# Moving one small store between queues and adding unread products at the end of a row-maximum kernel

## Chip, cores, metric

One core of a Trainium2 chip. The metric is device time in microseconds (us) of one execution; medians are over executions on the chip. Profiles are single executions; "the span" is the profiled part of one, about 1.8 us shorter than its time.

## The reference

```python
def setup_inputs():
    return {"x": np.random.randn(8192, 8192).astype(np.float32)}

def reference(x):
    return np.linalg.norm(x, ord=np.inf, axis=1)   # the largest |x| of each row
```

It is 268 MB in and 32 KB out.

## The kernel before

SyncE loads pairs of rows for each of the 128 partitions into a ring of three 64 KB buffers, and VectorE reduces them to one value for each row, in columns of `res`. The last rows come in shrinking pieces, shared by VectorE, ScalarE (absolute value) and GpSimd (maximum). At the end TensorE turns the columns of `res` into lines by a transpose against the identity, ScalarE copies them out of PSUM, and two stores write them out: 60 row tiles as "pairs", and the last 4 as "ones", which contain the row tile that is reduced last. So that TensorE's clock is up for these transposes, products that nobody reads (`ps_warm`) are issued near the end; `WARM` gives their lengths in blocks of 128 columns by tile (negative) or by piece of the last tile.

```python
WARM = {-2: (4, 4, 4), -1: (4,), 0: (4,), 1: (2,)}
# ...
    def warm(after, widths):
        for w in widths:
            not_before(
                keep(nc.tensor.matmul(
                    ps_warm[:, : w * P], lhsT=ident,
                    rhs=ident.unsqueeze(1).to_broadcast([P, w, P]), start=True, stop=True,
                )),
                after, "not before this piece",
            )
# ... in the loop over the pieces of all tiles
            if final:                                    # the last piece of the last tile
                for r in range(2):
                    keep(nc.scalar.copy(sb_pairs[:, :, r], ps_pairs[r]))
                absmax(res[:, R - 1 :], last)            # the last reduction, VectorE
            elif u == len(TILES) - 1:                    # an earlier piece h of the last tile
                if h == 0:
                    # ... two transposes into ps_pairs
                red = shared(last, w_last + n_part, buf, w, g)
                n_part += 1 + len(g)
                warm(red, WARM.get(h, ()))
# ... after the loop
    nc.tensor.transpose(ps_ones, res[:, X_ONE:], ident)
    keep(nc.scalar.copy(sb_ones, ps_ones))
    keep(nc.scalar.dma_start(
        out=out[X_ONE * P :].rearrange("(r p) -> r p", p=P), in_=sb_ones
    ))
    nc.sync.dma_start(
        out=out[: X_ONE * P].rearrange("(g p r) -> g p r", p=P, r=2), in_=sb_pairs
    )
```

## Time and profile before

| | before |
|---|---|
| time | 628.23 us (3 runs, 628.09 to 628.24) |
| DMA engines busy | 99% of the span, 428 GB/s |
| VectorE busy | 536.8 us (86%) |
| last reduction ends | 623.87 us into the span |
| from there to the end of the span ("the tail") | 2.75 us |

The lines are shown in the prediction. They are read in this order: the chain of work that ended last, to see that loads and reductions make up 99% of it; the timeline of the last 4 us, to see the serial path of the tail and what lies beside it; the granted clock in narrow slices, to see what TensorE ran at. The tail serves below as the measure of each change: the load stream ahead of it ends at a different moment in each execution (623.49 to 623.87 us in the ten profiles without a changed last store), which hides tenths of a microsecond in the total time but not in the tail.

### The profile page before, as it was taken

What the parts mean: (1) busy time and instruction counts of PE and PEld (TensorE: products, weight loads), DVE (VectorE), ACT (ScalarE), POOL (GpSimd) and SP (SyncE); (2) the same over time, 40 slices, a digit from 0 to 9 for tenths busy, and PEclk for the clock granted to TensorE, in tenths of its full rate; (3) what the DMA queues carried; (4) which work ended last, traced back from release to release, by engine and by line L of the source; (5) the groups of instructions that cost most, each with busy time, mean ns of one, the idle gap of its engine ahead of it and who ended that gap; (6) DMA issues with size and microseconds to landing.
All of it is one profiled execution on the core that took longest, in us unless ns stands there. A gap on an engine that the chain in (4) does not pass through costs nothing.

```text
span 626.6 us, 212 instructions
## 1 busy us (share of the span) xinstructions
PE 8.1 (1%) x15; PEld 3.0 (0%) x15; DVE 536.8 (86%) x40; ACT 15.6 (2%) x13; POOL 14.6 (2%) x16
## 2 busy tenths in 40 slices
PE   0000000000000000000000000000000000000005
PEld 0000000000000000000000000000000000000001
DVE  1938988889888899888898888988889888899888
ACT  0000000000000000000000000000000000000044
POOL 0000000000000000000000000000000000000026
PEclk9999999999999999999999999999999999999999
DMA  8999999999999999999999999999999999999997
GB/s 368 435 469 402 469 402 469 402 469 402 464 406 464 406 456 414 431 439 427 443 410 460 406 464 402 469 402 469 402 464 406 464 406 464 406 460 410 439 410 291
DMA packets 5669, 268.47 MB, mean 428 GB/s; under 512 B 643, under 2 KB 933, under 8 KB 1317
## 3 DMA queue, kind: packets, MB, share of 16 engines
q1 hardware_dynamic: 5661, 268.47, 99.2%
q10 hardware_dynamic: 8, 0.00, 0.0%
HBM read 268.44 MB, written 0.03 MB: 428 GB/s over the span
## 4 chain that ended last, share of the span: by engine, by line
DMA 71%; DVE 28%; SPq 0%; issue 0%; PE 0%; ACT 0%; DVEq 0%
DMA ring<-in_x_dram 71%; DVE res L75 28%; DVE last L75 1%; SPq L147 0%; PE ps_ones L189 0%; ACT sb_ones L190 0%; DVEq L75 0%
## 5 line engine op out<-in xcount | busy, mean ns | idle before, releaser
L75 DVE TENSOR_REDUCE res<-ring 128x2 f32<-128x16384 f32 (+1 forms) x32 | 525.4, 16420 | 86.8 <-DMA ring<-in_x_dram 86.8
L97 ACT ACTIVATE ring<-ring 128x3712 f32<-128x3712 f32 (+7 forms) x8 | 13.5, 1712 | 575.9 <-DMA ring<-in_x_dram 572.6
L82 POOL TENSOR_REDUCE part<-ring 128x1 int32<-128x3712 int32 (+3 forms) x4 | 10.1, 2563 | 586.0 <-ACT ring L97 586.0
L118 PE MATMUL ps_warm<-ident 128*128 128x512 f32 (+1 forms) x12 | 7.5, 764 | 614.5 <-DVE part L75 613.2
L118 PEld LDWEIGHTS ps_warm<-ident 128*128 128x128 f32 x12 | 2.7, 258 | 618.4 <-issue 615.3
L75 DVE TENSOR_REDUCE part<-ring 128x1 f32<-128x800 f32 (+1 forms) x2 | 5.5, 2748 | 0.1
L75 DVE TENSOR_REDUCE last<-ring 128x1 f32<-128x2176 f32 (+4 forms) x5 | 5.3, 1115 | 0.1
L82 POOL TENSOR_REDUCE last<-ring 128x1 int32<-128x1696 int32 (+3 forms) x4 | 3.3, 842 | 0.5 <-ACT ring L97 0.4
L110 ACT ACT_TABLE_LOAD x1 | 1.3, 1283 | 31.6 <-DVE res L75 31.6
L104 POOL MEMSET ident<- 128x128 f32 x1 | 0.2, 206 | 21.5 <-DVE res L75 21.5
L75 DVE TENSOR_REDUCE res<-last 128x1 f32<-128x425 f32 x1 | 0.6, 595 | 0.1
L161 ACT COPY sb_pairs<-ps_pairs 30x128 f32<-30x128 f32 x2 | 0.4, 252 | 0.0
L82 POOL TENSOR_REDUCE res<-part 128x1 int32<-128x3 int32 x2 | 0.4, 200 | 0.1
L167 PE MATMUL ps_pairs<-ident,res 128*30 128x128 f32 x2 | 0.4, 272 | 0.0
L189 PE MATMUL ps_ones<-ident,res 128*4 128x128 f32 x1 | 0.3, 348 | 1.7 <-DVE res L75 1.7
masks.py:199 POOL TENSOR_SCALAR_AFFINE_SELECT ident<-ident 128x128 f32<-128x128 f32 x1 | 0.3, 295 | 0.1
L190 ACT COPY sb_ones<-ps_ones 4x128 f32<-4x128 f32 x1 | 0.3, 255 | 1.5 <-PE ps_ones L189 1.5
L167 PEld LDWEIGHTS ps_pairs<-ident,res 128*30 128x30 f32 x2 | 0.2, 106 | 0.6 <-issue 0.6
L110 ACT ACTIVATE ident<-ident 128x1 f32<-128x1 f32 x1 | 0.2, 203 | 0.0
L211 POOL MEMSET const-float32-0.0<- 128x1 f32 x1 | 0.1, 99 | 0.2 <-issue 0.2
L211 POOL MEMSET const-bfloat16-1.0<- 128x1 bf16 x1 | 0.1, 102 | 0.0
L211 POOL MEMSET const-uint8-127<- 128x1 uint8 x1 | 0.1, 102 | 0.0
(2 smaller groups left out, 0.2 us busy)
## 6 DMA issues: line engine op xcount, KB each, us to landing
ring<-in_x_dram SPq DMA_DIRECT2D x3, 4096.0 KB, 21.6
ring<-in_x_dram SPq DMA_DIRECT2D x1, 1936.0 KB, 35.4
ring<-in_x_dram SPq DMA_DIRECT2D x1, 976.0 KB, 37.3
ring<-in_x_dram SPq DMA_DIRECT2D x1, 512.0 KB, 38.1
ring<-in_x_dram SPq DMA_DIRECT2D x30, 40.8
ring<-in_x_dram SPq DMA_DIRECT2D x1, 272.0 KB, 38.3
last<-in_x_dram SPq DMA_DIRECT2D x1, 208.0 KB, 38.3
ring<-in_x_dram SPq DMA_DIRECT2D x1, 192.0 KB, 38.3
```

The lines of the kernel that those rows point to most:

```text
L75: return keep(nc.vector.tensor_reduce(out=dst, in_=src, axis=X, op=MAX, apply_absolute_value=True,))
L82: keep(pool.add_instruction(mybir.InstTensorReduce(name=nc.get_next_instruction_name(), ins=[pool.lower_ap(src.bitcast(INT32))], outs=[poo ...
L97: keep(nc.scalar.activation(buf[:, a : a + c], buf[:, a : a + c], ABS))
L104: not_before(nc.gpsimd.memset(ident, 0.0), after, "not before the first row is in")
L110: keep(nc.scalar.activation(ident[:, :1], ident[:, :1], ABS)),
L118: keep(nc.tensor.matmul(ps_warm[:, : w * P], lhsT=ident, rhs=ident.unsqueeze(1).to_broadcast([P, w, P]), start=True, stop=True,)),
L161: keep(nc.scalar.copy(sb_pairs[:, :, r], ps_pairs[r]))
L167: keep(nc.tensor.transpose(ps_pairs[r], both[:, :, r], ident))
L189: nc.tensor.transpose(ps_ones, res[:, X_ONE:], ident)
L190: keep(nc.scalar.copy(sb_ones, ps_ones))
L211: nc = _bacc.Bacc("TRN2", target_bir_lowering=False, num_devices=1)
```

## The change

The pairs' store goes from SyncE's queue to ScalarE's, ahead of the last store in program order. Two more unread products keep TensorE busy until just before the last transpose.

```diff
-WARM = {-2: (4, 4, 4), -1: (4,), 0: (4,), 1: (2,)}
+WARM = {-2: (4, 4, 4), -1: (4,), 0: (4,), 1: (2,), 2: (2,), 4: (1,)}
@@ in the loop, final piece
                 for r in range(2):
                     keep(nc.scalar.copy(sb_pairs[:, :, r], ps_pairs[r]))
+                keep(nc.scalar.dma_start(
+                    out=out[: X_ONE * P].rearrange("(g p r) -> g p r", p=P, r=2), in_=sb_pairs
+                ))
                 absmax(res[:, R - 1 :], last)
@@ after the loop
-    nc.sync.dma_start(
-        out=out[: X_ONE * P].rearrange("(g p r) -> g p r", p=P, r=2), in_=sb_pairs
-    )
```

## The prediction

> **What bounds the kernel now.** I read the page first (busy shares, then the chain of work that ended last), because it says whether the edited lines stand on the path at all.
>
> ```profile
> PE 8.1 (1%) x15; PEld 3.0 (0%) x15; DVE 536.8 (86%) x40; ACT 15.6 (2%) x13; POOL 14.6 (2%) x16
> ...
> DMA ring<-in_x_dram 71%; DVE res L75 28%; DVE last L75 1%; SPq L147 0%; PE ps_ones L189 0%; ACT sb_ones L190 0%; DVEq L75 0%
> ```
>
> The second line is the chain by tile and line: loads into the ring take 71% of it and the VectorE reductions that free the ring 28%. The DMA engines are busy 99% of the span at 428 GB/s, reading 268.44 MB; that stream alone is 268.44 / 0.428 = 627 us. Nothing in the edit touches it: the first added product waits for a reduction that ends at 622.3 us. So only the last 4 us can move, and I read those from the timeline, restricted to narrow windows, to see instructions singly.
>
> ```profile
> 622.42 0.41 ACT L161 COPY sb_pairs<-ps_pairs 30x128 f32<-30x128 f32 x2
> 622.85 0.42 SPq L194 DMA_DIRECT2D out_dram<-sb_pairs  x1
> 623.27 0.59 DVE L75 TENSOR_REDUCE res<-last 128x1 f32<-128x425 f32 x1
> 623.92 0.08 PEld L189 LDWEIGHTS ps_ones<-ident,res 128*4 128x4 f32 x1 [2.05 <-DVE res L75]
> 623.92 0.35 PE L189 MATMUL ps_ones<-ident,res 128*4 128x128 f32 x1 [1.65 <-DVE res L75]
> 624.31 0.26 ACT L190 COPY sb_ones<-ps_ones 4x128 f32<-4x128 f32 x1 [1.48 <-PE ps_ones L189]
> 624.60 0.55 ACTq L191 DMA_DIRECT2D out_dram<-sb_ones  x1
> ```
>
> Columns: start and duration in us, engine, line, operation, and in brackets the idle time before it with its releaser. The reader should see one serial chain: last reduction (ends 623.86), transpose on TensorE (ends 624.27), copy on ScalarE (ends 624.57), issue of the last store (ends 625.15), then its landing, then the end barrier to 626.6. Beside it lies the pairs' store on SyncE, issued at 622.85, 1.75 us before the last store. The waits of SyncE's queue, the last 10 us only, say which store the program waits for:
>
> ```profile
> SPq L222 <- DMA out_dram<-sb_ones: 2.3, 1, 2.3
> ```
>
> It is the last store, not the pairs'. The table of DMA issues gives the pairs' store 1.4 us to landing, so it is down at 622.85 + 1.4 = 624.3, before the last store is even issued. In the trace's semaphore records the last store's four increments end at 625.81, 1.21 us after its issue began, and 0.8 us of end barrier follows.
>
> The last view is the granted clock in slices of 0.4 us. Columns: PE, PEld, DVE, ACT and POOL busy, then clock, DMA share, GB/s.
>
> ```profile
> 622.80:623.20 0.40, 0.00 (x0) 0.00 (x0) 0.38 (x1) 0.03 (x1) 0.15 (x1) 1.00 0.00 0
> 623.20:623.60 0.40, 0.00 (x0) 0.00 (x0) 0.33 (x1) 0.00 (x0) 0.00 (x0) 1.00 0.00 0
> 623.60:624.00 0.40, 0.07 (x1) 0.08 (x1) 0.27 (x1) 0.00 (x0) 0.00 (x0) 0.99 0.30 77
> 624.00:624.40 0.40, 0.27 (x1) 0.01 (x1) 0.00 (x0) 0.09 (x1) 0.00 (x0) 0.50 0.00 0
> ```
>
> TensorE is idle from 622.27 on, and its clock falls to half at about 623.99 (the slice's 0.99 leaves 0.4 x 0.02 = 8 ns at half), just after the last transpose begins at 623.92. So that transpose runs mostly at the half clock: 348 ns in the trace, against 272 ns for each transpose of the pairs at full clock.
>
> **What the Trainium skill says.**
> - "TensorE: Matmul & The Clock Gate", section "What's actually happening": the clock gate decides by free-running windows of 3413 ns and halves the clock after idle. The trace agrees in size: the full clock is recorded from 617.16 to 623.99 us, 6.83 us, two such windows. In the second (620.58 to 623.99) the products fill 1.8 of 3.4 us and the clock still falls, so the page's "idle window" is not the whole rule here.
> - Same page, "Part 4: PE-mode transpose": the full clock "doesn't engage" for transposes, about 275 ns in a kernel. The 272 ns agrees in size; the 348 ns of the last transpose says that the clock does matter, unless that duration is only modelled. ScalarE's copy, which waits for it, starts 0.39 us after the transpose did, so at least its end is real.
> - Same page, "Architectural detail: the array is 16× 32×32, not 1× 128×128": ScalarE takes instructions strictly in order. So an issue placed ahead of the last copy holds it up if it lasts long enough. The trace has ScalarE in program order throughout.
> - "DMA: Bandwidth & Descriptors", section "Issuing engines are not separate DMA queues": another issuing engine saves only the sequencer's issue time. Here SyncE's issue is 0.42 us and ScalarE's 0.55 us, both with idle time around them.
>
> **The change, part by part.**
>
> 1. The pairs' store leaves SyncE. Removed: one issue of 0.42 us at 622.85 to 623.27. SyncE then waits until the last store lands at 625.81; 2.5 us lie between. On the path: 0.
>
> 2. It goes to ScalarE, after the two copies that end at 622.83. Cost by the only row of ScalarE's queue: 0.55 us, from 622.86 to about 623.41. ScalarE is next wanted at 624.31 (at 624.23 if the transpose gets faster). Slack: 624.23 - 623.41 = 0.8 us. On the path: 0. Landing shifts from 624.3 by at most the 0.13 us of longer issue to about 624.4, before the last store's issue at about 624.5. On the path: 0.
>
> 3. The last store becomes the second issue on ScalarE's queue instead of the first. If part of the 0.55 us is a first-use cost, up to 0.55 - 0.42 = 0.13 us is saved on the path. I give it little: SyncE's first issue, at 0.74 us, took 0.40 us, no longer than its later ones. Its expectation: 0.02 us.
>
> 4. The added products. The two-block product after piece 2 waits for the reduction that ends at 622.3 (piece 3's begins at 622.21, and completion is signalled about 0.1 us later). In the profile a two-block product is a pair of records spanning 0.70 us (621.57 to 622.27), so it runs 622.36 to 623.1. The one-block product after piece 4 waits for the reduction that ends at 623.18, so it starts at about 623.25. Its length: four-block pairs span 1.12 us and two-block 0.70, that is 0.21 per block, so 0.49 us, to 623.74. The last transpose can start at 623.92, when its input is reduced. Slack: 0.18 us. Nothing of it is on the path if the clock stays full. At half clock its time would double at worst, about 1 us, to 624.2, and would push the transpose back by 0.3 us.
>
> 5. What they buy. Busy time in the window before the fall goes from 1.8 to 1.8 + 0.7 + 0.5 = 3.0 of 3.4 us, and the idle stretch before the last transpose from 1.65 us to about 0.2. If that keeps the clock full, the transpose takes 272 in place of 348 ns: 0.076 us off the path. I give it 60%, as the windows run free of the kernel and the rule is not known to me: 0.05 us expected.
>
> Sum: -0.05 - 0.02, plus 0.02 for the chance that a product delays the transpose, is -0.05 us; a mode of -0.08 us and a small tail above zero. From 628.23 that is 628.16.
>
> **The rivals.**
> - The added products delay the last transpose: the slack of 0.18 us is an estimate, and the product after piece 4 stands directly ahead of the transpose in TensorE's order. For: the margin is thin. Against: the clock is full until 623.99 even without them. It would make 628.3 to 628.5.
> - The pairs' store holds up ScalarE or the last store's landing, now that both share a queue. For: they are issued 1.7 us apart at most and a small store needs 1.2 to 1.4 us. Against: the first is down before the second is issued, and the second's own data come 0.8 us later. It would add a few tenths: 628.4.
> - The move pays more than I say: ScalarE's queue is slow only at its first use, and the transpose also wins. It would make 628.0.
> - The whole change is hidden, and only noise is seen: 628.1 to 628.3, the spread of the runs before.
>
> **Range and chances.** 628.16 us, range 627.9 to 628.4: below lies the sum of both gains (0.21) and a little chance, above a delay of 0.1 to 0.2 and the spread between sessions (0.15 within one). A change of 2% is 12.6 us, three times the 4 us that the edit can reach; only a disturbed load stream could give that, so same 0.98, faster 0.01, slower 0.01.
>
> **What would show it right or wrong.** Step 1 and 2: in the timeline the pairs' store on ScalarE's queue from about 622.85, for about 0.55 us, with the last copy still released by TensorE, not by an issue. Step 3: the last issue's duration, 0.55 or 0.42 us. Step 4: the last added product ending before the last transpose starts, with that transpose still 0.06 us after the last reduction. Step 5: clock 1.00 past 624.3 and a transpose near 272 ns. The end of the last reduction should stay near 623.9. The prediction is wrong if the load stream's end moves by more than 0.3 us, if ScalarE's issue takes over 1.3 us, or if the transpose waits for a product.

## The result

| | before | after |
|---|---|---|
| median, same rounds | 628.24 us (6 runs, 627.88 to 628.37) | 628.04 us (6 runs, 627.87 to 628.52) |
| ratio | | 0.9999, 95% interval 0.9986 to 1.0012 |
| last reduction ends (profile) | 623.87 us | 623.54 us |
| tail (profile) | 2.75 us | 2.62 us |

A ratio is the mean time of one kernel's runs over that of the other's of the same rounds, so it is not quite the ratio of the medians. Executions over 1.5% slower than the fastest of the same kernel are left out of the means. By time the two kernels are the same.

The timeline of the changed kernel, last 4 us, in the columns explained in the prediction:

```profile
622.55 0.64 ACTq L162 DMA_DIRECT2D out_dram<-sb_pairs  x1
...
622.90 0.49 PE L118 MATMUL ps_warm<-ident 128*128 128x128 f32 x2 [0.20 <-DVE last L75]
622.94 0.60 DVE L75 TENSOR_REDUCE res<-last 128x1 f32<-128x425 f32 x1
...
623.59 0.27 PE L192 MATMUL ps_ones<-ident,res 128*4 128x128 f32 x1 [0.20 <-DVE res L75]
623.90 0.26 ACT L193 COPY sb_ones<-ps_ones 4x128 f32<-4x128 f32 x1 [1.38 <-PE ps_ones L192]
624.19 0.26 ACTq L194 DMA_DIRECT2D out_dram<-sb_ones  x1
```

The store of the pairs is on ScalarE's queue, and the copy at 623.90 is still released by TensorE. Two durations fell: the last transpose from 0.35 to 0.27 us, and the issue of the last store from 0.55 to 0.26 us. The granted clock of the same kernel, in slices (PE, PEld, DVE, ACT, POOL busy, then clock, DMA share, GB/s):

```profile
623.60:624.00 0.40, 0.26 (x1) 0.07 (x1) 0.00 (x0) 0.10 (x1) 0.00 (x0) 1.00 0.04 10
624.00:624.40 0.40, 0.00 (x0) 0.00 (x0) 0.00 (x0) 0.16 (x1) 0.00 (x0) 1.00 0.00 0
```

It stays at 1.00 where the kernel before had fallen to 0.50. The waits of SyncE's queue name the same last wait as before, the last store's landing:

```profile
SPq L222 <- DMA out_dram<-sb_ones: 2.5, 1, 2.5
```

The tail can be taken apart at the starts of its steps; the landing is the last of the store's increments in the semaphore records.

| step of the tail | before | after | difference |
|---|---|---|---|
| last reduction's end to transpose's start | 0.056 us | 0.055 us | 0 |
| transpose's start to copy's start | 0.385 us | 0.308 us | -0.077 us |
| copy and hand-over to the issue | 0.285 us | 0.286 us | 0 |
| issue's start to landing | 1.213 us | 1.164 us | -0.049 us |
| landing to the end of the span | 0.807 us | 0.807 us | 0 |
| sum | 2.746 us | 2.620 us | -0.126 us |

An issue that is shorter by 0.285 us brings the landing forward by only 0.05 us: most of the long issue lies beside the transfer's own delay. In the DMA records the store's first data move 0.795 us after the issue began before, 0.742 us after.

The remaining 0.33 us of the two spans' difference is the earlier end of the load stream, which the edit does not touch.

### The profile page after: what moved, and what is told of

Its sections match the earlier page's. It is cut to its first block, busy times and chain, and to the rows that moved or that the text cites. A ratio compares the mean times of both kernels' runs of the same rounds, so it can differ in the third digit from the quotient of the medians.

```text
span 626.2 us, 219 instructions
## 1 busy us (share of the span) xinstructions
PE 9.3 (1%) x19; PEld 3.7 (1%) x19; DVE 536.8 (86%) x40; ACT 15.6 (2%) x13; POOL 14.6 (2%) x16
## 4 chain that ended last, share of the span: by engine, by line
DMA 71%; DVE 28%; SPq 0%; issue 0%; PE 0%; ACT 0%; DVEq 0%
DMA ring<-in_x_dram 71%; DVE res L75 28%; DVE last L75 1%; SPq L147 0%; PE ps_ones L192 0%; ACT sb_ones L193 0%; DVEq L75 0%
## 5 line engine op out<-in xcount | busy, mean ns | idle before, releaser
L118 PE MATMUL ps_warm<-ident 128*128 128x512 f32 (+2 forms) x16 | 8.8, 674 | 614.4 <-DVE part L75 612.9
```

The lines of the kernel that those rows point to most:

```text
L118: keep(nc.tensor.matmul(ps_warm[:, : w * P], lhsT=ident, rhs=ident.unsqueeze(1).to_broadcast([P, w, P]), start=True, stop=True,)),
```

## Experiments

My theory after the result: the tail has two separate gains, the clock (from the products) and the second use of ScalarE's queue (from the move), and the scatter of the stream hides both. Rivals: the move or the products cause both; or the faster median has its source in the stream. All kernels gave correct results. The experiments ran on three chips (0, 12 and 13 by the record). "Against" gives the median of the kernel before, run beside each one on the same chip; profiles of different chips are compared by their tails.

### The changed kernel again

No edit. 

> The changed kernel once more, as the yardstick of this chip. In the trace, the tail from the end of the last VectorE reduction to the end of the span should be 2.6 us again (before: 2.75 us), whatever the load stream does; the last store's issue 0.26 us, the last transpose 0.27 us at full clock. Theory (tail gain of 0.12 us, hidden in the scatter of the load stream): ratio to before 0.9998, interval across 1. Rival (the median's 0.2 us is real and comes from somewhere else too): ratio below 0.9996 and a last reduction that ends 0.2 to 0.3 us earlier again.

Median 628.07 us (5 runs) against 628.21 us (9 runs), ratio 0.9998 (0.9985 to 1.0010). Its tail is 2.624 us, with transpose 0.272 us and last issue 0.264 us. Its last reduction ends at 623.73 us, between the 623.54 and 623.87 of the first two profiles, so the earlier end is scatter. The tail repeats within 4 ns.

### The store alone

```diff
-WARM = {-2: (4, 4, 4), -1: (4,), 0: (4,), 1: (2,), 2: (2,), 4: (1,)}
+WARM = {-2: (4, 4, 4), -1: (4,), 0: (4,), 1: (2,)}      # as before
```

> Only the pairs' store moved, products as before. Theory (two separate gains): the last store's issue falls to 0.26 us and its landing after the start of the issue from 1.21 to 1.16 us; the clock falls to half near the last transpose as before, so the transpose takes 0.35 us; tail 2.70 us. Rival (the short issue is an effect of the fuller clock or of the shorter wait): issue stays 0.55 us.

Half of it came as expected. Median 628.03 us against 628.21 us, ratio 0.9997 (0.9985 to 1.0010). The timeline of this kernel:

```profile
623.69 0.27 PE L192 MATMUL ps_ones<-ident,res 128*4 128x128 f32 x1 [1.64 <-DVE res L75]
...
624.28 0.26 ACTq L194 DMA_DIRECT2D out_dram<-sb_ones  x1
```

The issue is short, as the theory has it. But the transpose also takes 0.27 us, with the old products and 1.64 us of idle TensorE ahead of it, and the tail is 2.622 us, all of the gain. The granted clock says why:

```profile
624.80:625.20 0.40, 0.00 (x0) 0.00 (x0) 0.00 (x0) 0.00 (x0) 0.00 (x0) 0.98 0.02 5
625.20:625.60 0.40, 0.00 (x0) 0.00 (x0) 0.00 (x0) 0.00 (x0) 0.00 (x0) 0.50 0.00 0
```

Here the clock falls at 625.19 us, 1.2 us after the transpose, not at 623.99 us. So either the move keeps the clock up, which has no visible means, or the moment of the fall is not the kernel's.

### The products alone

The edit to `WARM` on the kernel before; the pairs' store stays on SyncE.

> Only the products added, the pairs' store stays on SyncE. Theory: clock full past 624.3 us, last transpose 0.27 us, its wait on ScalarE's side 0.08 us shorter; last issue 0.55 us and landing 1.21 us as in the kernel before; tail 2.67 us. Rival (the move is what keeps the transpose fast): transpose 0.35 us.

```profile
623.73 0.27 PE L189 MATMUL ps_ones<-ident,res 128*4 128x128 f32 x1 [0.20 <-DVE res L75]
...
624.32 0.55 ACTq L191 DMA_DIRECT2D out_dram<-sb_ones  x1
```

As expected on every point: transpose 0.272 us, issue 0.547 us, landing 1.209 us after it, tail 2.665 us. Median 628.09 us, ratio 0.9998 (0.9984 to 1.0011). The short issue belongs to the move alone.

### An early first use of ScalarE's queue

```diff
+    scratch = single.tile([n_ones, P], FP32)
+    keep(nc.scalar.dma_start(out=scratch, in_=x[:n_ones, :P]))   # at the start, never read
```
on the kernel before.

> The kernel before with one extra load of 4 x 128 numbers on ScalarE's queue at the very start, which nothing reads. Theory (the first DMA of a program on ScalarE's queue costs more, however early): the extra load's issue takes 0.55 to 0.64 us at the start and the last store's issue falls to 0.26 us. Rival (it is recency: a queue or its instructions not used for hundreds of us are slow again): last issue 0.55 us. Tail 2.70 us under the theory, 2.75 us under the rival.

The timeline, first and last:

```profile
0.74 0.55 ACTq L127 DMA_DIRECT2D scratch<-in_x_dram  x1
...
623.55 0.27 PE L192 MATMUL ps_ones<-ident,res 128*4 128x128 f32 x1 [1.65 <-DVE res L75]
...
624.14 0.26 ACTq L194 DMA_DIRECT2D out_dram<-sb_ones  x1
```

The long issue stays with the first DMA of the queue, 623 us earlier, and the last store's falls to 0.264 us. Recency is out. The tail, 2.696 us, agrees with the expected 2.70 us only by luck: the transpose was quick here too (0.273 us), and 0.064 us were added between landing and end (0.871 us instead of 0.807 us). The instruction records show why: SyncE waits for the DMAs' semaphores one after the other, and with this extra DMA one such check, at 625.38 us, is still to come after the last landing, where the kernel before has none. The three candidates at the end, which also have one DMA more, have two to four such checks there, and their stretch from landing to end grows in step, by 0.06 us each (0.93 us with two, 1.00 with three, 1.05 with four). The median, 628.48 us (5 runs, 628.03 to 628.65), is not shorter; ratio 1.0002 (0.9990 to 1.0015).

### A long product ahead of the transpose

```diff
-WARM = {-2: (4, 4, 4), -1: (4,), 0: (4,), 1: (2,), 2: (2,), 4: (1,)}
+WARM = {-2: (4, 4, 4), -1: (4,), 0: (4,), 1: (2,), 2: (2,), 4: (4,)}
```

> The changed kernel with the product after piece 4 made four blocks long instead of one. It tests the first rival of the prediction, that a product can stand ahead of the last transpose. Theory: it starts 0.64 us before the last reduction ends and lasts 1.12 us at full clock, so the transpose starts 0.48 us after that end instead of 0.055 us: tail 2.62 + 0.43 = 3.05 us. Rival (TensorE takes the transpose ahead, or the product is broken off): tail stays 2.62 us.

```profile
623.05 1.13 PE L118 MATMUL ps_warm<-ident 128*128 128x512 f32 x2 [0.20 <-DVE last L75]
623.09 0.60 DVE L75 TENSOR_REDUCE res<-last 128x1 f32<-128x425 f32 x1
...
624.01 0.27 PE L192 MATMUL ps_ones<-ident,res 128*4 128x128 f32 x1
```

The rival of the prediction exists: the transpose waits for the product, and its line no longer has a releaser, since TensorE was not idle. The tail is 2.89 us, so the product costs 0.27 us, not the 0.43 us expected. The product's two records end at 624.18 us, but the transpose starts at 624.01 us: records of consecutive products overlap, and 0.17 us of a record's end do not hold up the next one. Median 628.36 us (4 runs) against 627.99 us, ratio 1.0007 (0.9991 to 1.0022).

### No products

`WARM = {}` on the changed kernel. 

> The changed kernel without any unread product. Theory (a transpose costs what the granted clock makes it cost): the clock stays at half, two transposes of the pairs start about 0.21 us apart instead of 0.109 us, so the last one takes about 0.27 + 0.11 = 0.38 us and ScalarE's copy starts 0.415 us after it instead of 0.308: tail 2.73 us. Rival (the clock doesn't matter to a transpose, the 348 ns of the profile before was only a modelled end): copy after 0.31 us, tail 2.62 us.

```profile
623.57 0.37 PE L192 MATMUL ps_ones<-ident,res 128*4 128x128 f32 x1 [9.75 <-DVE res L75]
623.98 0.25 ACT L193 COPY sb_ones<-ps_ones 4x128 f32<-4x128 f32 x1 [1.52 <-PE ps_ones L192]
```

The copy starts 0.410 us after the transpose (expected 0.415), the tail is 2.716 us (expected 2.73). A transpose without the products costs 0.10 us more, and the kernel before, with 348 ns, had been caught in the middle of a fall. The clock slices of this run mislead:

```profile
623.60:624.00 0.40, 0.34 (x1) 0.05 (x1) 0.00 (x0) 0.02 (x1) 0.00 (x0) 1.00 0.00 0
```

They print 1.00, because the trace holds no clock record at all: without a rise there is no fall to record, and the view shows 1.00 where it has nothing. (The traces of the three candidates, which have no products either, hold none too.) The duration of the transpose is the better witness. Median 628.05 us (4 runs) against 627.99 us, ratio 1.0001 (0.9988 to 1.0015).

### Where the clock falls

In each trace of this table the full clock lasts 6.83 or 10.24 us, two or three times 3.41 us. So each fall or hold of the clock can be set against how much of the 3.41 us before it TensorE was in products or transposes. The windows are counted from the moment that the trace's clock record rises; each starts where the last one ended. The share is worked out from the product records in the trace.

| kernel (products) | clock full, us | windows: share filled | transpose starts, takes |
|---|---|---|---|
| before (old) | 617.16 to 623.99 | 0.66 held, 0.48 fell | 623.92, 348 ns |
| store alone (old) | 618.36 to 625.19 | 0.81 held, 0.16 fell | 623.69, 271 ns |
| early first use (old) | 616.05 to 626.29 | 0.75 and 0.53 held, 0.08 fell | 623.55, 273 ns |
| after (new) | 617.23 to 627.47 | 0.70 and 0.77 held, 0.00 fell | 623.59, 271 ns |
| after again (new) | 616.08 to 626.32 | 0.78 and 0.74 held, 0.22 fell | 623.79, 272 ns |
| products alone (new) | 616.95 to 627.19 | 0.66 and 0.82 held, 0.06 fell | 623.73, 272 ns |

The windows start at another moment in each execution, with no regard to the kernel, and in these six profiles the clock falls at the end of one filled to 0.48 or less and holds at 0.53 or more. The long product and the last store on SyncE's queue fit too (0.66 and 0.88, 0.73 and 0.71 held; 0.12 and 0.00 fell). But the share is not the only reading: in all these windows and those of the two kernels below, the longest idle stretch of TensorE is 1.62 us or less where the clock held and 1.64 us or more where it fell. No run here tells a rule of share from a rule of idle stretch. With the old products, sliding such a window over the traces of before and of the store alone gives an estimate, if the limit is near a half: about one start in ten puts a window under half full with its end close enough to the last transpose to slow it. With the new products no window that ends before the transpose is filled below 0.58 in any of the five traces. Two further kernels put this to the test.

The first keeps only the products that bring the clock up, on the changed kernel: `WARM = {-2: (4, 4, 4), -1: (4,)}`.

> The changed kernel with only the products that bring the clock up, none after the last tile begins. Theory (the clock falls at the end of a 3413 ns window that products fill to less than about half): some window that ends before the last transpose is nearly empty whatever its phase, so the clock is at half again before 623.5 us, the transpose takes 0.37 us and the copy starts 0.41 us after it: tail 2.72 us. Rival (the clock falls only after a long idle stretch, or by chance): transpose 0.27 us, tail 2.62 us.

```profile
617.20:620.60 3.40, 1.87 (x6) 0.56 (x4) 3.32 (x3) 2.17 (x2) 2.96 (x3) 1.00 0.98 405
620.70:624.10 3.40, 0.27 (x1) 0.08 (x1) 2.92 (x5) 1.48 (x6) 2.00 (x4) 1.00 0.49 180
...
624.00:624.40 0.40, 0.05 (x1) 0.00 (x0) 0.00 (x0) 0.25 (x1) 0.00 (x0) 0.62 0.00 0
```

The expected slow transpose did not come: it took 272 ns, tail 2.615 us (one run, 628.11 us, state unknown; its comparison had a median of 628.16 us over 9 runs). The third slice shows the reason, a fall at about 624.1 us (0.62 means 0.3 of the 0.4 us at half), just behind the transpose, which starts at 623.77. Counted from the record's rise at 617.27 us, the first window was filled to 0.53 and held, the second to 0.08 and fell at 624.10. The two bounds on the share stand, but my "whatever its phase" was too strong: this start missed the harmful ones narrowly, and the run shows no slowed transpose.

The second is the store alone once more, edit as above. 

> The store moved, old products, a second look at where the clock's windows fall. Theory (their phase is free, and only a window that ends in the 0.3 us around the last transpose is both under half full and early enough to matter, about one in ten): most likely a transpose of 0.27 us again, with the clock's fall at another place than 625.19 us; tail 2.62 us. Rival (the old products make the clock fall near 624.0 us as a rule): transpose 0.35 us, tail 2.70 us.

The clock is full from 617.51 to 624.34 us (windows filled to 0.74, held, and 0.35, fell), again at another place. The transpose starts at 623.62 us and takes 271 ns; tail 2.617 us (one run, 627.98 us, state unknown). Of four looks at the old products, one met a slowed transpose. That is in keeping with an estimate of one in ten, but four looks don't fix a share.

### The last store from SyncE's queue

```diff
-    keep(nc.scalar.dma_start(
+    keep(nc.sync.dma_start(
         out=out[X_ONE * P :].rearrange("(r p) -> r p", p=P), in_=sb_ones
     ))
```
on the changed kernel. 

> The changed kernel with the two stores' queues swapped: pairs on ScalarE's, the last one on SyncE's queue, which has issued 39 loads. Theory (a queue that has been used is as quick, whichever it is): issue to first data 0.74 us, landing 1.17 us, tail 2.62 us. Rival (SyncE's queue is slower for a store, as its store of the pairs in the kernel before started 0.85 us after its issue began): data after 0.85 us, tail 2.73 us.

```profile
624.51 0.33 SPq L194 DMA_DIRECT2D out_dram<-sb_ones  x1
```

First data 0.768 us after the issue began, landing after 1.193 us, tail 2.642 us: nearer the theory (0.74, 1.17, 2.62) than the rival (0.85, 2.73). A used queue is nearly as quick whichever it is; ScalarE's is better by 0.02 us here. Median 628.20 us (4 runs) against 628.16 us, ratio 0.9999 (0.9985 to 1.0013).

### Three candidates for a shorter tail

The first takes the transpose and ScalarE's copy off the last path. The first three single rows (row tiles) are transposed and stored early, and the last one is turned by VectorE. All three candidates also drop the products (`WARM = {}`) and put the last row's maxima into a new tile `fin`; the cuts show the rest.

```diff
-    nc.tensor.transpose(ps_ones, res[:, X_ONE:], ident)      # three columns now, at piece 1
-    keep(nc.scalar.copy(sb_ones, ps_ones))                   # with its store, after the pairs' store
-    keep(nc.scalar.dma_start(out=out[X_ONE * P :]..., in_=sb_ones))
+    keep(nc.vector.transpose(fin_t, fin))                    # fin[:, 0] holds the last row's maxima
+    keep(nc.scalar.dma_start(
+        out=out[(R - 1) * P :].rearrange("(q i) -> q i", i=32), in_=fin_t[0:P:32, :]
+    ))
```

> A candidate that takes TensorE and ScalarE's copy off the last path: the first three single rows are transposed and stored early, the last one is turned by VectorE in 32 x 32 blocks and stored as four pieces of 128 bytes; no products. Theory (the path after the last reduction is what counts): transpose start, transpose and copy (0.055 + 0.308 + 0.256 us) give way to about 0.06 + 0.15 us, so tail 2.62 - 0.41 = 2.2 us and about 0.4 us less time, ratio to before 0.9992. Rival (a store close behind two others on ScalarE's queue lands later): tail 2.5 us or more.

```profile
623.58 0.26 ACTq L169 DMA_DIRECT2D out_dram<-sb_ones  x1
623.66 0.21 DVE L201 STREAM_TRANSPOSE fin_t<-fin 128x32 f32<-128x32 f32 x1
623.91 0.58 ACTq L202 DMA_DIRECT2D out_dram<-fin_t  x1
```

The first half worked: the last issue starts 0.28 us after the last reduction, not 0.65 us. The second did not: the issue takes 0.58 us, the data come 1.22 us and the landing 1.61 us after its start (0.74 and 1.16 us for the store that it replaces), and 1.00 us lie between landing and end, not 0.81, because of three semaphore checks of SyncE that come after the landing. Tail 2.89 us, median 628.32 us (5 runs) against 627.99 us, ratio 1.0005 (0.9993 to 1.0018). I took the store 0.33 us ahead of it for the cause and tested that:

```diff
+                keep(nc.scalar.copy(sb_ones, ps_ones))       # before the pairs' copies
+                keep(nc.sync.dma_start(out=out[X_ONE * P : (R - 1) * P]..., in_=sb_ones))
                 # ... the pairs' copies and their store
-                keep(nc.scalar.copy(sb_ones, ps_ones))
-                keep(nc.scalar.dma_start(out=out[X_ONE * P : (R - 1) * P]..., in_=sb_ones))
```

> The first candidate with its two early stores pulled apart: the three single rows are copied first and stored from SyncE's queue, the pairs after them on ScalarE's, about 1.15 us before the last store instead of 0.33 us. Theory (the last store of c1 waited behind the store 0.33 us before it): its issue falls from 0.58 to 0.26 us, its data start 0.75 us after the start of the issue instead of 1.22 us, tail 2.3 to 2.4 us, ratio to before 0.9994. Rival (four pieces of 128 bytes, or a third store, are slow in themselves): data again 1.2 us after, tail 2.8 us.

```profile
623.12 0.64 ACTq L169 DMA_DIRECT2D out_dram<-sb_pairs  x1
...
624.26 0.58 ACTq L202 DMA_DIRECT2D out_dram<-fin_t  x1
```

That theory fell. With 1.14 us between the issues, the last one takes 0.577 us and its data come after 1.218 us, as in the first candidate; tail 2.94 us, median 628.60 us (5 runs) against 628.16 us, ratio 1.0005 (0.9991 to 1.0018). The store is slow in itself. Whether that is its 128-byte pieces, its source on every 32nd partition, or the first use of something other than the queue stays open.

The other candidate stores the last row straight from its column, with no turning:

```diff
-    keep(nc.vector.transpose(fin_t, fin))
     keep(nc.scalar.dma_start(
-        out=out[(R - 1) * P :].rearrange("(q i) -> q i", i=32), in_=fin_t[0:P:32, :]
+        out=out[(R - 1) * P :].rearrange("(p o) -> p o", o=1), in_=fin[:, :1]
     ))
```

> A second candidate: as the first, but the last row's 128 values are stored straight from their column, as 128 pieces of 4 bytes, with no turning at all. Theory: 0.64 us of transpose and copy go, the many small pieces add 0.3 us (eight for each DMA engine): tail 2.3 us. Rival (small writes land much later): issue to landing over 1.8 us instead of 1.17 us, tail 2.7 us or more.

Its table of DMA issues, with the time to landing in the last column:

```profile
out_dram<-sb_pairs ACTq DMA_DIRECT2D x1, 30.0 KB, 1.5
...
out_dram<-fin ACTq DMA_DIRECT2D x1, 0.5 KB, 6.9
```

The rival, and worse: 512 bytes in pieces of 4 take 6.9 us to land, against 1.5 us for 30 KB in pieces of 1 KB. Median 633.28 us (4 runs) against 627.99 us, ratio 1.0084 (1.0070 to 1.0098), the only difference that the times themselves resolve. No version beat the two kernels; the store alone has the same tail as the whole change in both of its profiles (2.622 and 2.617 us), in neither of which the transpose was slowed.

## Why the prediction was right, and where its parts were not

The forecast of 628.16 us, within 2%, held: 628.04 us, ratio 0.9999. The hit says little, since the range of 627.9 to 628.4 us also holds every median of the kernel before. By its own steps:

- **Bound, and reach of the edit: right.** The loads set the time up to the last reduction, and what the edit moved lies in the tail, -0.126 us in the two profiles. By its own words the prediction would be wrong if the load stream's end moved by more than 0.3 us, and between the two profiles it moved by 0.33 us. But the changed kernel alone ended it at 623.54 and 623.73 us, so that limit was tighter than the scatter; it was not the step that failed.
- **Steps 1 and 2: right.** SyncE's freed issue changed nothing. ScalarE's new issue took 0.64 us instead of the 0.55 us taken from the other store, and the pairs landed at 624.04 us, still ahead of the last issue at 624.19 us. The copy was released by TensorE, with 0.7 us of slack.
- **Step 3: mis-sized.** It gave a first-use cost on ScalarE's queue 0.02 us, because SyncE's first issue was not slow. The early first use shows the cost: 0.55 us for the first issue, 0.26 us for the last. Its term is -0.05 us on the path, and it comes in each look at a moved store. The step also bounded the gain by the difference between the two queues' issues, 0.13 us; the issue shrank by 0.285 us, but its length is mostly not on the path.
- **Step 4: right in effect, its slack too small.** The product after piece 4 ended 0.20 us before the transpose by its record, and the long product shows some 0.17 us more, since TensorE is free before a record ends.
- **Step 5: right mechanism, wrong baseline.** 0.076 us was predicted for a transpose at full clock and 0.077 us was measured between the two profiles. It misread the window's sum, though: by the records 1.63 of its 3.41 us are filled, not 1.8, and 2.6 with the new products, not 3.0. And "So that transpose runs mostly at the half clock" took one execution for the kernel. In the three other looks at the old products the transpose took 271 to 273 ns. With an estimate of one start in ten, and 0.077 us for a slowed one, the products are worth about 0.01 us on average, not 0.05.
- **The sum** of -0.05 us is near the -0.06 us that these corrected terms give (-0.05 and -0.01) because the two errors cancel, which is luck. (628.23 - 0.05 is 628.18, not the 628.16 given.) The times cannot check it: the medians of the kernel before alone, in four sets of rounds on at least three chips, lay between 627.99 and 628.24 us.

Of the rivals, a product ahead of the transpose is real but needs a longer product, two stores in each other's way were not seen in the change, and "the move pays more than I say" came true in kind.

## What to carry to other kernels

A tail of a few microseconds is best judged from the end of the last bounding operation to the end of the span, step by step, because it repeats within some nanoseconds while the total scatters by tenths of a microsecond. A duration in one profile that hangs on a free-running clock is a draw and not a property: look at a second execution before crediting a change with it. The first DMA of ScalarE's queue is better spent on a store that nobody waits for; here that brought the last landing forward by 0.05 us. It also pays to look at what the program still checks after its last landing: here each further semaphore check cost 0.06 us.

## What the Trainium skill lacked or had wrong

- "TensorE: Matmul & The Clock Gate", section "What's actually happening": it names an idle window as what halves the clock. Here windows filled to 0.48 or less by products let it fall and windows filled to 0.53 or more held it; in the fullest one that let it fall, the longest idle stretch was 1.65 of 3.41 us, so a wholly idle window is not needed.
- Same page, "Part 4: PE-mode transpose": it says that the full clock doesn't engage for transposes. Here (float32, and if these transposes, MATMUL in the trace, run in the mode that the page means) the last one took 271 to 273 ns at full clock and 373 ns without products.
- No page that I read has a first-use cost of ScalarE's DMA queue: the first issue took 0.55 us for 4 pieces and 0.62 to 0.64 us for 30, the second, for the same four pieces as in the kernel before, 0.26 us, with the landing 0.05 us sooner. (Last stores of other shapes, in the candidates, took 0.37 and 0.58 us to issue.)
- "DMA: Bandwidth & Descriptors", section "Specifications": it asks for pieces of 512 bytes for full rate, but gives no landing time for smaller ones. Here 128 pieces of 4 bytes took 6.9 us to land, and 4 pieces of 128 bytes from every 32nd partition 1.61 us, against 1.16 us for 4 pieces of 512 bytes.
- No page that I read says that a trace without any clock record, read through the slices, looks like a full clock: the kernel without products shows 1.00 beside its 373 ns transpose.
